# A step of dense matmuls between the copies of a recurrent state and its transpose

## Chip, cores and metric

The kernel runs on one core of a Trainium2 chip. The metric is the device time of one execution in microseconds. Before the change the median of 3 runs is 1598.35 us (1597.43 to 1599.26). The chip's engines are named as in the profile: PE is TensorE (PEld its weight loads), DVE is VectorE, ACT is ScalarE, POOL is GpSimd and SP issues the DMAs.

## The reference

One layer of a hybrid decoder for 1024 tokens of width 1024, in float32: a norm, one input projection, two head groups side by side (retention on 4 heads of 128, RWKV-7 on 8 heads of 64), an output projection, a SwiGLU feed-forward part, a gated embedding and a last norm. What matters here is RWKV-7, whose state of 64 x 64 per head is updated token after token:

```
def step(state, inp):
    r_t, w_t, k_t, v_t, kk_t, b_t = inp
    sa = jnp.einsum('bhvk,bhk->bhv', state, -kk_t)
    state = (state * w_t[:, :, None, :] + sa[..., None] * b_t[:, :, None, :]
             + v_t[..., None] * k_t[:, :, None, :])
    return state, jnp.einsum('bhvk,bhk->bhv', state, r_t)
...
_, y = lax.scan(step, jnp.zeros((B, H, N, N), jnp.float32),
                (tm(r), tm(decay), tm(k), tm(v), tm(kk), tm(kk * a)))
```

The rest is mostly dense products, among them `proj = hn @ w_in`, `mixed @ w_o` and `silu(hf @ w_gate) * (hf @ w_up)`.

## The kernel before

**Dense work.** Each large product of 128 x 512 outputs is a row of matmuls `d` with 512 columns. An operand is split into a high and a low part (`hi`, `lo`, line 250 on ScalarE and line 251 on GpSimd or VectorE), so that every 128 rows of the inner dimension take three matmuls: high x high, high x low, low x high. Such a group of three is called a piece here; `dense` (line 258) is a generator that emits one piece at each call. The tokens are done in two halves of 512.

**The RWKV groups.** `rwkv_group(p, hf)` does two heads (p = 0 to 3) of one half (hf = 0, 1), so there are eight groups in a row. Its 512 tokens are cut into 8 chunks of 64 (`NU`). A group goes through stages: `prep` and `ops` (factors), `A` (products `pb` and the inversion of a triangular matrix by 62 short VectorE instructions in turn, lines 646 and 648), `tok` (products `pk`, transposes `pq`), `mid` (first the products `psm`, whose results ScalarE copies to `hbd` and `Xb`, then `pw` with copies to `Wbd` and `Gbd`, then `pmq` and `pkh`), `chain`, and `fin` (norm of the output, transposes `py` and `pyt`, store of `Y`).

**The chain** (lines 742 to 758) carries the state over the 8 chunks, each step on the one before. A step u writes `pZ` with two products, one from `Vbd` and `KA`, one from the old state `Sn` and `BA`. Then the new state, which stands in two 64 x 64 blocks of `pZ`, is copied to `STb`, one block by ScalarE (line 751) and one by VectorE (line 752). TensorE transposes it (`tr`, line 754, a matmul with the identity, line 196, into `pS`), and ScalarE copies that with a scale into the next `Sn` (line 756). The last chunk of the second half needs no new state, so the transpose runs 8 x 4 + 7 x 4 = 60 times. While a group is in its chain, the next group is in stage `A`: its inversion shares VectorE with the chain's copies.

**The order.** `weave` (line 117) writes the program. A group's generator hands back a stage and a wait, `yield "chain", CHW`; the group's next step is due when the planner's own clock has gone on by the wait times 1.58 in the first half (`WAIT`) and 1.98 in the second (`WAIT1`), and until then `weave` emits dense pieces, or retention tasks that are due. That clock counts a matmul of 512 columns as 512 / 2.4 = 213.3, a piece as 640. Before, the step's products, copies, transpose and copy out are emitted at once, and `CHW = 900` then asks for 1422 (first half) or 1782 (second half), which is three pieces in both. Retention tasks (`rtp`, `rsc`, `rU`, `rY`, `ryt`, lines 793 to 878) are woven in the same way.

What `weave` writes isn't yet the order on the chip: a list scheduler then places each instruction on its engine by priorities and a model of when its inputs are ready. An instruction whose inputs it takes to be late is put behind others that were written after it. Each engine runs its row in that order. SP's row holds all loads and stores, those of weights (`st`) too.

Of the kernel before, what the change touches and what calls it, by code (L numbers as in the profile page):

```python
# [95 lines left out]
MIDW = 9676  # L96
MIDS = 1378
TOKW = 1156
CHW = 900
RLD = 3770  # L100
RROT = 3633
RST = 6253
# [76 lines left out]
def tile_hybrid_layer(ctx: ExitStack, tc: tile.TileContext, I, out):  # L179
# [7 lines left out]
    def mm(ps, lhsT, rhs, start, stop, more=False):  # L187
        n = math.prod(rhs.shape[1:])
        pe[0] += n / 2.4 if rhs.dtype == F32R else 2 * max(107.0, n / 1.2)
        m = nc.tensor.matmul(ps, lhsT, rhs, start=start, stop=stop, skip_group_check=more)  # L190
        tail["mm"] = m.ins
        return m

    def tr(ps, x):
        pe[0] += 109.0
        return nc.tensor.transpose(ps, x, ident)
# [29 lines left out]
    def psa(name):  # L226
        return psr.tile([P, 512], F32, tag="ra", name=name, bufs=2)
# [125 lines left out]
    with ExitStack() as s1:  # L353
# [197 lines left out]
        def flat(t):  # L551
            return t.rearrange("p h t -> p (h t)")
# [3 lines left out]
        def rwkv_group(p, hf):  # L556
# [186 lines left out]
            for u in range(NU):  # L743
                z = pZ[u % 2][:, u // 2]
                first = hf == 0 and u == 0
                mm(flat(z), flat(Vbd[:, u]), flat(KA[:, u]), start=True, stop=first)
                if not first:
                    mm(flat(z), state[p], flat(BA[:, u]), start=False, stop=True)
                if hf == 0 or u < NU - 1:
                    st = STb[:, u % 2]  # L750
                    act(st[0:64, 0, :], z[0:64, 0, :], AF.Copy)
                    V.tensor_copy(st[64:128, 1, :], z[64:128, 0, :])
                    ps = psa("pS")[:, 0:P]
                    tr(ps, flat(st))
                    Sn = sm.tile([P, P], F32, tag=f"S{p}" if u == NU - 1 else "S", name="Sn", bufs=1 if u == NU - 1 else 2)
                    act(Sn, ps, AF.Copy, scale=PC[:, u:u + 1])
                    state[p] = Sn
                yield "chain", CHW

# [537 lines left out]
        for h in range(2):  # L1297
            for k in range(KT):
                tasks[f"mix{h}{k}"] = (mix_load(h, k), 0, ["wo0" if h else "x0free", f"ret{k}{h}" if k < 4 else f"group{k - 4}{h}"])
        weave([(f"group{p}{hf}", rwkv_group(p, hf), need[p]) for hf in range(2) for p in range(4)],  # L1300
              tasks, dg, count, pe, done)

# [242 lines left out]
```

## Time and profile before

| | |
|---|---|
| median of 3 runs | 1598.35 us |
| the profiled execution | 1598.74 us |
| its span, first to last instruction | 1597.0 us |
| TensorE busy | 1497.2 us, 94% |
| VectorE, ScalarE, GpSimd busy | 1203.1, 722.4, 512.7 us |
| mean granted TensorE clock | 0.986 |
| chains of the eight groups | within 186 to 892 us |

The busy time of TensorE is no measure of its speed, since its matmuls overlap and their ends are modelled; what counts is where it stands idle and why. A wait in the profile names the instruction that stood still, and behind the arrow the one that released it.

### The profile page before, as it was taken

What the parts mean: (1) busy time and instruction counts of PE and PEld (TensorE: products, weight loads), DVE (VectorE), ACT (ScalarE), POOL (GpSimd) and SP (SyncE); (2) the same over time, 40 slices, a digit from 0 to 9 for tenths busy, and PEclk for the clock granted to TensorE, in tenths of its full rate; (3) what the DMA queues carried; (4) which work ended last, traced back from release to release, by engine and by line L of the source; (5) the groups of instructions that cost most, each with busy time, mean ns of one, the idle gap of its engine ahead of it and who ended that gap; (6) DMA issues with size and microseconds to landing.
All of it is one profiled execution on the core that took longest, in us unless ns stands there. A gap on an engine that the chain in (4) does not pass through costs nothing.

```text
span 1597.0 us, 21675 instructions
## 1 busy us (share of the span) xinstructions
PE 1497.2 (94%) x7328; PEld 1220.0 (76%) x7328; DVE 1203.1 (75%) x2466; ACT 722.4 (45%) x1442; POOL 512.7 (32%) x389
## 2 busy tenths in 40 slices
PE   6999899998888889989889999999999999999997
PEld 5777768776677767767768877778888888888897
DVE  7668895969889696894875545768888888886675
ACT  6755435353545647445344324543333333334554
POOL 7411111121321122324223340455555555570000
PEclk9999999999999999999999999999999999999998
DMA  6544242242544555335233546332223222331222
GB/s 199 175 154 166 96 129 84 89 152 78 174 133 145 189 165 190 96 105 155 87 127 113 171 119 188 115 121 85 92 90 90 91 93 86 119 93 56 83 91 75
DMA packets 108767, 194.09 MB, mean 122 GB/s; under 512 B 12272, under 2 KB 16496, under 8 KB 108656
## 3 DMA queue, kind: packets, MB, share of 16 engines
q1 hardware_dynamic: 108656, 192.71, 38.0%
q8 instruction: 58, 0.95, 0.2%
q14 instruction: 53, 0.43, 0.1%
HBM read 151.24 MB, written 41.42 MB: 121 GB/s over the span
## 4 chain that ended last, share of the span: by engine, by line
PE 57%; DVE 23%; ACT 7%; DMA 6%; issue 4%; POOL 2%; SPq 0%; ACTq 0%; DVEq 0%; POOLq 0%
PE d L190 31%; PE pd L190 13%; PE pg L190 6%; DVE tmp L646 4%; DVE R L648 3%; DMA st<-in_w_gate_dram 2%; POOL lo L251 2%; DMA st<-in_w_up_dram 1%; DVE lo L251 1%; ACT hi L250 1%; DVE Dm L640 1%; DVE inv L599 1%; PE pkh L190 1%; PE pb L190 1%; ACT BA L685 1%
## 5 line engine op out<-in xcount | busy, mean ns | idle before, releaser
L190 PE MATMUL d<-hT,hi 128*128 128x512 f32 x1408 | 452.0, 401 | 4.1 <-ACT hi L250 4.1
L251 POOL TENSOR_TENSOR lo<-st,hi 128x512 fp32r<-128x512 f32 x173 | 241.8, 1399 | 590.6 <-ACT hi L250 531.3
L190 PE MATMUL d<-x,hi 128*128 128x512 f32 x960 | 319.7, 408 | 8.9 <-ACT x L339 8.0
L190 PEld LDWEIGHTS d<-hT,hi 128*128 128x128 f32 x1408 | 263.5, 192 | 54.9 <-ACT hi L250 5.6
L250 ACT ACTIVATE hi<-st 128x512 fp32r<-128x512 f32 x298 | 187.0, 628 | 258.2 <-PE d L190 96.4
L190 PE MATMUL d<-hT,lo 128*128 128x512 f32 x704 | 279.8, 398 | 5.9 <-DVE lo L251 3.4
L190 PE MATMUL pd<-ring 128*128 128x512 f32 x948 | 260.4, 389 | 0.0
L190 PEld LDWEIGHTS d<-x,hi 128*128 128x128 f32 x960 | 177.1, 192 | 43.3 <-ACT x L339 8.0
L190 PEld LDWEIGHTS pd<-ring 128*128 128x128 f32 x948 | 177.9, 188 | 37.1 <-ACT rm L1145 0.2
L190 PE MATMUL d<-x,lo 128*128 128x512 f32 x480 | 192.9, 402 | 2.8 <-POOL lo L251 2.4
L190 PEld LDWEIGHTS d<-hT,lo 128*128 128x128 f32 x704 | 134.2, 191 | 38.3 <-DVE lo L251 6.3
L251 DVE TENSOR_TENSOR lo<-st,hi 128x512 fp32r<-128x512 f32 x125 | 115.7, 927 | 55.9 <-ACT hi L250 54.9
L1147 DVE TENSOR_TENSOR x<-x,pd 128x512 f32<-128x512 f32 x180 | 118.6, 679 | 26.9 <-PE pd L190 26.9
L251 POOL TENSOR_TENSOR ring<-xr,ring 128x512 fp32r<-128x512 f32 x53 | 73.2, 1386 | 146.5 <-ACT ring L250 67.3
L250 ACT ACTIVATE ring<-rm 128x512 fp32r<-128x512 f32 x87 | 53.8, 629 | 131.3 <-DVE rm L1080 83.8
L190 PEld LDWEIGHTS d<-x,lo 128*128 128x128 f32 x480 | 92.0, 192 | 23.1 <-POOL lo L251 4.7
L646 DVE TENSOR_TENSOR tmp<-Dt,R 128x248 f32<-128x248 f32 (+30 forms) x248 | 89.5, 361 | 3.2
L648 DVE TENSOR_TENSOR R<-R,tmp 128x248 f32<-128x248 f32 (+30 forms) x248 | 83.8, 338 | 3.3
L190 PE MATMUL d<-mix,hi 128*128 128x512 f32 x256 | 82.1, 400 | 0.9 <-ACT hi L250 0.9
L251 DVE TENSOR_TENSOR ring<-rm,ring 128x512 fp32r<-128x512 f32 x65 | 58.4, 902 | 13.0 <-ACT ring L250 12.1
L250 ACT ACTIVATE ring<-xr 128x512 fp32r<-128x512 f32 x57 | 34.9, 625 | 73.8 <-PE pd L190 72.6
L190 PEld LDWEIGHTS d<-mix,hi 128*128 128x128 f32 x256 | 48.1, 192 | 10.8 <-ACT hi L250 1.3
(315 smaller groups left out, 2393.7 us busy)
## 6 DMA issues: line engine op xcount, KB each, us to landing
st<-in_w_gate_dram SPq DMA_DIRECT2D x88, 256.0 KB, 2.9
st<-in_w_up_dram SPq DMA_DIRECT2D x88, 256.0 KB, 2.9
st<-in_w_in_dram SPq DMA_DIRECT2D x86, 256.0 KB, 2.9
xr<-in_w_down_dram SPq DMA_DIRECT2D x44, 256.0 KB, 2.7
retd<-rt SPq DMA_DIRECT2D x32, 256.0 KB, 2.5
rr<-retd SPq DMA_DIRECT2D x32, 256.0 KB, 3.4
st<-in_w_o_dram SPq DMA_DIRECT2D x32, 256.0 KB, 3.0
rkvd<-rkvt SPq DMA_DIRECT2D x24, 256.0 KB, 2.1
```

The costliest lines, as they stand in the source:

```text
L190: m = nc.tensor.matmul(ps, lhsT, rhs, start=start, stop=stop, skip_group_check=more)
L250: act(hi, src, AF.Copy)
L251: return (eng or V).tensor_tensor(out=lo, in0=src, in1=hi.bitcast(F32), op=ALU.subtract)
L599: V.reciprocal(out=inv, in_=inv)
L640: V.tensor_tensor(out=Dm, in0=d0v[:, 0].rearrange("p u t -> p t u").unsqueeze(2).broadcast_to([P, 32, 4, NU]), in1=d0v[:, 1].rearrange("p ...
L646: V.tensor_tensor(out=tmp[:, :, 0:i], in0=Dt[:, i:i + 1, 0:i].broadcast_to([P, 8, i]), in1=R[:, :, i:i + 1].broadcast_to([P, 8, i]), op=AL ...
L648: V.tensor_tensor(out=R[:, :, 0:i], in0=R[:, :, 0:i], in1=tmp[:, :, 0:i], op=ALU.subtract)
L685: act(dst(h)[h * C:(h + 1) * C, j::2, :], pqv[j * C:(j + 1) * C, :, h, :], AF.Copy)
L1147: V.tensor_tensor(out=dst, in0=dst, in1=ps, op=ALU.subtract if name == "P4" else ALU.add)
```

## The change

Behind the two copies the chain's step now ends with a wait of its own, and the wait behind the transpose is shorter. By the planner's clock `CHT = 400` asks for 632 in the first half, one piece, and for 792 in the second, two pieces. `CHW = 500` asks for 790 and 990, two pieces in both. A step so takes three pieces in the first half, as before, and four in the second for three.

```
-CHW = 900
+CHT = 400
+CHW = 500
...
                     st = STb[:, u % 2]
                     act(st[0:64, 0, :], z[0:64, 0, :], AF.Copy)
                     V.tensor_copy(st[64:128, 1, :], z[64:128, 0, :])
+                    yield "chain", CHT
                     ps = psa("pS")[:, 0:P]
                     tr(ps, flat(st))
```

Every engine has the same instructions as before. Their rows are the same up to the first chain and from the last retention transpose on, and differ nearly everywhere between. (The numbers of the lines are one higher from line 100 on, and two higher from line 754 on.)

First place: TensorE in the fourth step of the last group's chain, before and with the change (`pZ<-BA,Sn` is the product with the old state, `pS<-cst,STb` the transpose, `d` dense matmuls, `ryt` a retention transpose).

```order
L190 MATMUL pZ<-KA,Vbd 128x128
L190 MATMUL pZ<-BA,Sn 128x128
L196 MATMUL ryt<-cst,rr 128x128 x4
L190 MATMUL d<-hT_5519,hi 128x512
L196 MATMUL pS<-cst,STb 128x128
L190 MATMUL d<-hT_5519,hi 128x512
L190 MATMUL d<-hT_5519,lo 128x512
L190 MATMUL d<-hT_5519,hi 128x512 x2
L190 MATMUL d<-hT_5519,lo 128x512
```

```order
L191 MATMUL pZ<-KA,Vbd 128x128
L191 MATMUL pZ<-BA,Sn 128x128
L191 MATMUL d<-hT_5511,hi 128x512 x2
L191 MATMUL d<-hT_5511,lo 128x512
L191 MATMUL d<-hT_5511,hi 128x512 x2
L191 MATMUL d<-hT_5511,lo 128x512
L197 MATMUL pS<-cst,STb 128x128
L191 MATMUL d<-hT_5511,hi 128x512 x2
L191 MATMUL d<-hT_5511,lo 128x512
L191 MATMUL d<-hT_5511,hi 128x512 x2
L191 MATMUL d<-hT_5511,lo 128x512
```

Before, one dense matmul and a retention transpose stood ahead of the state's transpose; in the steps around it, three dense matmuls. Now there are six in nearly every step of this group, and six behind it.

Second place: TensorE in stage `mid` of the third group of the second half, before (the next row is the first `pw`) and with the change; then ScalarE's row there with the change, from behind the first two copies to `hbd`.

```order
L190 MATMUL psm<-R,a_180 128x32 x4
L196 MATMUL rtp<-cst,rr 128x128 x3
L190 MATMUL d<-hT_5519,hi 128x512 x2
L196 MATMUL rtp<-cst,rr 128x128
L190 MATMUL psm<-Xd,hbd 128x32 x4
L190 MATMUL d<-hT_5519,lo 128x512
L190 MATMUL d<-hT_5519,hi 128x512 x2
L190 MATMUL d<-hT_5519,lo 128x512
L190 MATMUL d<-hT_5519,hi 128x512 x2
L190 MATMUL d<-hT_5519,lo 128x512
L190 MATMUL d<-hT_5519,hi 128x512 x2
L190 MATMUL d<-hT_5519,lo 128x512
```

```order
L191 MATMUL d<-hT_5511,lo 128x512
L191 MATMUL psm<-R,a_180 128x32 x4
L197 MATMUL rtp<-cst,rr 128x128 x4
L191 MATMUL psm<-Xd,hbd 128x32 x4
L197 MATMUL rtp<-cst,rr 128x128 x4
L191 MATMUL pw<-XR,Xb 128x128 x4
L191 MATMUL rsc<-rr 128x128 x4
L191 MATMUL pw<-XR,Xb 128x128 x4
L191 MATMUL pmq<-BA,Wbd 128x128 x4
L191 MATMUL pkh<-BA,Gbd 128x128 x2
L191 MATMUL rU<-rr 128x128 x3
L191 MATMUL pkh<-BA,Gbd 128x128
```

```order
L251 ACTIVATE mix<-st 128x512
L708 ACTIVATE hbd<-psm 32x4x32 x2
L251 ACTIVATE mix<-st 128x512
L831 ACTIVATE rr<-rtp,cst 128x512
L713 ACTIVATE Xb<-psm 32x4x32 x4
L831 ACTIVATE rr<-rtp 128x512
L724 ACTIVATE Wbd<-pw 64x4x64 x2
L724 ACTIVATE Gbd<-pw 64x4x64 x2
L724 ACTIVATE Wbd<-pw 64x4x64 x2
L724 ACTIVATE Gbd<-pw 64x4x64 x2
L611 ACTIVATE ta<-ta,par 128x512
L251 ACTIVATE hi<-st 128x512 x2
```

Before, dense matmuls `d` stand between the products of the stage. Now the whole stage, with tasks of a retention head (`rtp`, `rsc`, `rU`), stands in one row, and the dense product goes on behind it. The high part of its next weights (`hi<-st`) stands on ScalarE behind all copies of the stage, and the first copies of `psm` stand around two splits of `mix`, whose data is the output of earlier groups, read back from memory. Between `pyt` of the group before and this `psm` there were 36 dense matmuls, and now there are 23.

Third place: TensorE at the two transposes `rtp` of the third retention head of the second half, before and with the change; both transposes write the same PSUM bank, which ScalarE copies out between them (line 829).

```order
L190 MATMUL d<-hT_5519,hi 128x512 x2
L190 MATMUL d<-hT_5519,lo 128x512
L196 MATMUL rtp<-cst,rr 128x128 x8
L196 MATMUL pyt<-cst,yn 128x128
L190 MATMUL d<-hT_5519,hi 128x512 x2
```

```order
L197 MATMUL pq<-cst,AR 128x128 x4
L197 MATMUL rtp<-cst,rr 128x128 x3
L191 MATMUL d<-hT_5511,hi 128x512 x2
L191 MATMUL d<-hT_5511,lo 128x512
L191 MATMUL d<-hT_5511,hi 128x512 x2
L191 MATMUL d<-hT_5511,lo 128x512
L191 MATMUL d<-hT_5511,hi 128x512 x2
L191 MATMUL d<-hT_5511,lo 128x512
L191 MATMUL d<-hT_5511,hi 128x512 x2
L191 MATMUL d<-hT_5511,lo 128x512
L197 MATMUL rtp<-cst,rr 128x128 x4
L191 MATMUL psm<-R,a_180 128x32 x4
```

Before, the second four stood right behind the first four; now 12 dense matmuls are between.

## Rows read from the trace of the kernel before

**Rows 1.** The page's busy times by engine: us (share of the span) and instructions.
```profile
PE 1497.2 (94%) x7328; PEld 1220.0 (76%) x7328; DVE 1203.1 (75%) x2466; ACT 722.4 (45%) x1442; POOL 512.7 (32%) x389
```

**Rows 2.** TensorE's waits, 180 to 960 us: instruction <- releaser: us, times, longest.
```profile
PE pS L196 <- DVE STb L752: 18.2, 22, 1.7
...
PE ryt L196 <- ACT rr L871: 4.8, 2, 3.3
PE rtp L196 <- ACT rr L829: 4.2, 1, 4.2
```

**Rows 3.** Windows, fourth and eighth chain: length, each engine's busy us, clock, DMA.
```profile
451.00:482.00 31.00, 25.59 (x148) 19.36 (x146) 30.00 (x81) 12.63 (x35) 9.71 (x6) 1.00 0.34 109
...
868.00:892.00 24.00, 23.32 (x122) 18.43 (x121) 10.31 (x19) 9.11 (x23) 7.46 (x6) 1.00 0.38 119
```

**Rows 4.** Timeline, last group's fifth step: start, us, engine, line, operation [idle <- releaser].
```profile
881.63 0.39 PE L190 MATMUL pZ<-BA,Sn 128*128 128x128 f32 x2
...
881.77 0.70 PE L190 MATMUL d<-hT,hi 128*128 128x512 f32 x2
...
882.30 0.23 DVE L752 COPY STb<-pZ 64x64 f32<-64x64 f32 x1 [2.18 <-ACT STb L751]
882.31 0.40 PE L190 MATMUL d<-hT,lo 128*128 128x512 f32 x1
...
882.58 0.33 PE L196 MATMUL pS<-cst,STb 128*128 128x128 f32 x1
```

**Rows 5.** Timeline, a step of the first group at 207 us.
```profile
207.38 0.34 DVE L646 TENSOR_TENSOR tmp<-Dt,R 128x176 f32<-128x176 f32 x1
...
207.50 1.35 POOL L251 TENSOR_TENSOR lo<-st,hi 128x512 fp32r<-128x512 f32 x1 [10.21 <-ACT hi L250]
...
207.75 1.30 DVE L648 TENSOR_TENSOR R<-R,tmp 128x176 f32<-128x176 f32 x1
...
209.08 0.23 DVE L752 COPY STb<-pZ 64x64 f32<-64x64 f32 x1
...
209.37 0.33 PE L196 MATMUL pS<-cst,STb 128*128 128x128 f32 x1 [1.06 <-DVE STb L752]
```

**Rows 6.** TensorE's waits as in rows 2, 186 to 482 us, then 538 to 892.
```profile
PE pS L196 <- DVE STb L752: 12.0, 12, 1.7
...
PE pS L196 <- DVE STb L752: 6.2, 10, 1.2
```

**Rows 7.** Timeline, TensorE at the third middle stage of the second half.
```profile
702.87 0.60 PE L196 MATMUL pyt<-cst,yn 128*128 128x128 f32 x4
...
718.82 0.97 PE L190 MATMUL psm<-R,a 128*128 128x32 f32 x8
...
721.51 0.73 PE L190 MATMUL d<-hT,hi 128*128 128x512 f32 x2 [1.36 <-ACT hi L250]
...
722.64 1.08 PE L190 MATMUL psm<-Xd,hbd 128*128 128x32 f32 x8 [0.29 <-ACT hbd L707]
...
724.07 1.05 PE L190 MATMUL d<-hT,hi 128*128 128x512 f32 x2
...
725.35 1.05 PE L190 MATMUL d<-hT,hi 128*128 128x512 f32 x2
...
731.43 0.62 PE L190 MATMUL d<-hT,hi 128*128 128x512 f32 x2
...
732.11 0.62 PE L190 MATMUL d<-hT,hi 128*128 128x512 f32 x2
```

**Rows 8.** Timeline, ScalarE at the same place.
```profile
720.04 0.63 ACT L250 ACTIVATE mix<-st 128x512 fp32r<-128x512 f32 x1 [0.79 <-DMA st<-mixd]
...
721.49 1.11 ACT L707 ACTIVATE hbd<-psm 32x128 f32<-32x128 f32 x4
723.76 1.12 ACT L712 ACTIVATE Xb<-psm 32x128 f32<-32x128 f32 x4 [1.17 <-PE psm L190]
...
728.63 0.38 ACT L723 ACTIVATE Wbd<-pw 64x256 f32<-64x256 f32 x1 [1.62 <-PE pw L190]
```

More of the change, by code (lines that the diff above doesn't have):

```diff
@@ L98 @@
 TOKW = 1156
-CHW = 900
+CHT = 400
+CHW = 500
 RLD = 3770
@@ L752, in rwkv_group @@
                     V.tensor_copy(st[64:128, 1, :], z[64:128, 0, :])
+                    yield "chain", CHT
                     ps = psa("pS")[:, 0:P]
```

## Prediction

> **What bounds the kernel now.** I read the page's busy times first, then TensorE's waits, then the stretches in which the state's chain runs, and last the timeline of single steps. TensorE is busy for 1497.2 of the span's 1597.0 us [rows 1]. The change adds and drops no instruction on any engine; it only moves them, from the first product of the first chain to the last retention transposes, all of it between 180 and 960 us. So the time can change only by what TensorE stands idle, or runs at a lower clock, in that stretch. Its longest wait there is that of the state's transpose, which stands for VectorE's half of the copy, 18.2 us in 22 waits [rows 2]. The chain's stretches show the same: in the fourth group of the first half TensorE is busy for 25.59 of 31 us while VectorE is busy for 30, and in the last group of the second half for 23.32 of 24 us with VectorE at 10.31 [rows 3]. The chain hurts where VectorE is full.
>
> How one step runs. In the last group the product with the state starts at 881.63, the copies end at 882.53 and the transpose starts at 882.58; with three dense matmuls between there is nothing to wait for [rows 4]. At 207 us the same step, with four dense matmuls between in the order, still waits 1.06 us: the VectorE instruction ahead of the copy, a subtraction of the inversion (L648), takes 1.30 us where its neighbour takes 0.34, beside a GpSimd instruction of 1.35 us, and the copy begins at 209.08 [rows 5]. So the latency of an unhindered step is already covered by the one piece that the scheduler puts there by itself. What is left to gain is in copies that are late in VectorE's queue.
>
> What the idle times mean. A dense matmul is shown 0.40 us long, but three start in 0.68 us (731.43 to 732.11), one each 0.23 us [rows 7]. A wait is counted from the shown end, so a true delay is 0.17 us longer than its row. First half: 12.0 us in 12 waits [rows 6], with 12 x 0.17 that is 14.0. Second half: 6.2 in 10, so 7.9. The other 38 of the 60 transposes can hide up to 0.17 us each, 6.5 at most; I take 3.
>
> **The sum, part by part.**
>
> 1. Second half of the tokens. The planner needs two pieces for the new wait and two for the old one there (the section on the change), four a step for three. In the order of instructions, the dense matmuls between the product with the state and the transpose are, over the 28 steps after each group's first, 125 before and 170 now: 1.6 more a step, 0.37 us. The ten waits are 0.79 us each on average. With 0.37 us more cover they lose 3.7 us; with the three more (0.69 us) that most steps get, 6.9. I take 6, since the added three are the rule in the order and the mean comes from a few steps that get none, and 1 of the hidden delays: **-7** (ends -3 and -9). The pieces themselves cost nothing, as the dense work is the same in total; they are taken from the stretches between the chains. The chains end later, the last one by 54 dense matmuls (12 us), but the last retention transpose still comes at the same place in the dense work, and the output projection behind it too.
>
> The row on the late copy bears on a rule. The Trainium skill, page "SBUF — State Buffer", section "SBUF: two separate sides", says that VectorE and GpSimd share a pair of ports as an exclusive lock: a VectorE instruction with two SBUF inputs waits for a whole GpSimd instruction. The trace agrees with 1.30 us for 0.34 [rows 5]. By that rule a piece of 0.69 us covers about half of such a block, and the ten waits would give back no more than the 6.9 above.
>
> 2. First half. One piece for the new wait, two for the old one: three as before, and the scheduler had dense work in front of the transpose already. The counts fall, from 162 to 140 over 28 steps; without the outliers of 17 and 12, and of 8 and 5 in the same places, 133 and 127. That takes 0.05 to 0.18 us of cover from each step, so 12 waits grow by 0.6 to 2.2: **+1**. Ends: all waits go, because the copies fall elsewhere (-14), or all 28 steps pay 0.18 (+5).
>
> 3. The middle stage of the third group of the second half. Before, 12 dense matmuls stand between its first product (psm) and its first pw; now there is none from psm to the last pkh, and the next weights' high part stands on ScalarE behind all of the stage's copies (second place in the section on the change). Its cost: ScalarE's work up to there is four hbd (1.11), four Xb (1.12), eight Wbd and Gbd (3.04) and five copies of 128x512 (mix, mix, two retention copies, ta; 0.63 each, 3.15), 8.4 us [rows 8]. The mix copy between the hbd copies waits for a load; before it began 17.2 us after pyt (702.87 to 720.04) [rows 7, 8], and now psm comes some 3.0 us earlier after pyt, with 23 dense matmuls between for 36. TensorE's own products there are about 60 starts of 0.1 us (psm: eight in 0.97), 6.0 us. Idle: 8.4 + 3.0 - 6.0 = 5.4. After the gaps of 1.36 and 0.29 us the matmuls run at half pace there, three in 1.28 us (724.07 to 725.35) for 0.68, for two such pieces: the clock at 1.2 for 2.4 GHz, 1.2 us. That comes again, so 6.6, less what the place loses already (1.36 + 0.29 + 2 x 0.17 + 1.2 = 3.2): **+3.4**. Ends: 0, if the load is in time and copies overlap more; +10.6, if nothing overlaps and the clock falls twice (8.4 + 3.0 + 2 x 1.2 - 3.2).
>
> On the clock the rule and this row weigh the same way, but it is the reason why this stall is dear: the Trainium skill, page "TensorE: Matmul & The Clock Gate", section "What's actually happening", says that the throttled clock is the default and activity releases it.
>
> 4. The first group of the second half has the same in small: the last psm is now followed at once by eight pw where 10 dense matmuls stood. The Xb copies (1.12) are open: **+1** (0 to +2.7, with four Wbd and Gbd copies of 0.38).
>
> 5. Two retention transposes in one PSUM bank stood back to back and waited 4.2 us for the copy out [rows 2]. Now 12 dense matmuls (2.8 us) stand between: **-3** (0 to -4.4).
>
> 6. The other waits between 180 and 960 us fall anew, since the rows of each engine stand differently; single lines of them are about 5 us [rows 2]. Zero, with 5 us to either side.
>
> Sum: -7 + 1 + 3.4 + 1 - 3 = **-4.6 us**. The profiled execution took 1598.74 us (its span and 1.7 us around it), 0.4 above the median of the runs shown, 1598.35; against the median that gives 1593.8. A measurement of this kernel can tell about 0.2%, 3.2 us, from no change.
>
> **Rivals.**
>
> A. The wait moves along. The copy stands in VectorE's queue by the same scheduler that places the transpose, and where the transpose comes later, so may the copy. For it: the step at 207 us has one matmul more of cover than the one at 881 us, and waits all the same [rows 4, 5]; the block by GpSimd is longer than a piece. Against it: in the last group, with VectorE half idle, nothing moves the copy. Then term 1 is -2, the sum +0.4, the time 1598.8.
>
> B. The uncovered middle stages eat the gain. Place: terms 3 and 4. Without them the sum is -9. With both at their high ends (10.6 + 2.7) it is +4.3: 1602.7, slower. It decides from a net price of 9 us on for no gain, of 12.2 for slower by 0.2%. For it: in the order there is no other work for TensorE. Against it: ScalarE and TensorE do overlap in the same stage today, with 0.29 us left open before the second psm [rows 7].
>
> C. The first half gains too: the transpose has its own step now, and if half of its 14.0 us go, term 2 is -7 and the time 1585.8.
>
> **Chances and range.** Forecast 0.55 (its own range 1588 to 1599: the ends of terms 1, 3 and 5, hardly all on one side), A 0.20, B 0.15, C 0.10. Faster by over 0.2% means below 1595.2, which lies above the forecast's middle: 0.39 of the forecast's 0.55, C's 0.10 and 0.03 of A, 0.52. Within 0.2%: 0.14 of the forecast, 0.14 of A, 0.02 of B, 0.30. Slower: 0.02 of the forecast, 0.03 of A, 0.13 of B, 0.18. The range reaches from C to B: 1585 to 1603.
>
> **What would show it.** Right: the wait of the transpose for the copy falls from 6.2 to under 3 us in the second half and stays near 12 in the first; a TensorE gap of several us in the third group's middle stage, with a granted clock below 1 there; the wait of the retention transpose gone. Wrong: the second half still waits 5 us or more (A), first-half waits under 7 us (C), or gaps of over 9 us in the two middle stages (B).

## The result, and the profile after

The change made the kernel slower: 1613.33 us (median of 4 runs, 1612.57 to 1613.73) against 1598.8 us (4 runs, 1597.43 to 1604.58) beside it; the ratio is 1.0077, 95% interval 1.0051 to 1.0103. The prediction was 1593.8 us with a range to 1603. The profiled execution took 1612.57 us, its span is 1610.8 us, 13.8 more than in the profile before.

The busy line of the page after, to set against [rows 1], shows where it is not: TensorE's busy time grew by 3.3 us only.

```profile
PE 1500.5 (93%) x7328; PEld 1231.0 (76%) x7328; DVE 1213.6 (75%) x2466; ACT 722.3 (45%) x1442; POOL 509.2 (32%) x389
```

TensorE's waits after, first from 180 to 960 us (against [rows 2]), then from 180 to 540 and from 540 to 985 (against [rows 6]); us in total, times, longest:

```profile
PE pS L197 <- DVE STb L753: 20.4, 21, 2.2
PE pyt L197 <- DVE yn L781: 18.6, 5, 7.0
...
PE pS L197 <- DVE STb L753: 9.5, 10, 2.0
...
PE pyt L197 <- DVE yn L781: 16.4, 3, 7.0
PE pS L197 <- DVE STb L753: 10.9, 11, 2.2
```

The state's transpose waits as long as before, 20.4 for 18.2 us. In the second half, where I expected under 3 us, it is 10.9 for 6.2. And a wait is in the list that was not worth a line before: pyt, the transposes behind the output norm, stand 16.4 us for VectorE's yn in the second half (1.0 us before). The retention transpose's 4.2 us [rows 2] are gone, and so is ryt's line.

**Why the transpose still waits.** A step of the sixth group's chain after, on TensorE, VectorE and GpSimd:

```profile
684.87 1.33 POOL L1009 TENSOR_TENSOR g<-g,R 128x512 f32<-128x512 f32 x1 [1.57 <-DVE g L1008]
685.10 1.31 DVE L647 TENSOR_TENSOR tmp<-Dt,R 128x192 f32<-128x192 f32 x1
...
685.60 0.39 PE L191 MATMUL pZ<-BA,Sn 128*128 128x128 f32 x2
...
687.20 1.38 POOL L252 TENSOR_TENSOR lo<-st,hi 128x512 fp32r<-128x512 f32 x1 [1.00 <-ACT hi L251]
...
687.62 1.16 DVE L649 TENSOR_TENSOR R<-R,tmp 128x184 f32<-128x184 f32 x1
...
689.33 0.23 DVE L753 COPY STb<-pZ 64x64 f32<-64x64 f32 x1
...
689.61 0.33 PE L197 MATMUL pS<-cst,STb 128*128 128x128 f32 x1 [1.77 <-DVE STb L753]
```

Eight dense matmuls start between the product (685.60) and the transpose and are done 2.2 us behind it. The copy, though, starts 3.73 us behind it. VectorE isn't idle: it works through the next group's inversion (L647, L649), two of whose instructions take 1.31 and 1.16 us beside GpSimd's of 1.33 and 1.38, and through retention's states. The mean over the 28 steps of the second half shows it plainly. Between the product with the old state and the transpose stand 4.46 dense matmuls before and 6.07 after, 0.37 us more at 0.2275 us each (three start in 0.68 us [rows 7]); the copy starts 1.51 us behind that product before and 1.88 after, 0.37 us more too. In the first half, over the 28 steps that have an old state, both fall: 5.79 to 5.00 matmuls (0.18 us), and 2.03 to 1.83 us (0.20). On average the copy moved along with its transpose, both ways.

Moving along would cost nothing if all steps were alike. But a step whose copy is later than its cover stands still, and a step with more cover than it needs gives nothing back. Behind each group's first transpose there are 24 stretches from product to transpose in the second half. With TensorE's own work taken off they lose 10.2 us before and 15.3 after, and the growth is in the late steps: four stretches of over 1 us make 4.8 us before, six make 10.3 after. The step above is one of the six.

**Why pyt waits.** TensorE at the sixth group's output after, then VectorE's row of the norm behind py there, from the start of the square root to yn:

```profile
698.93 0.60 PE L197 MATMUL py<-cst,Y 128*128 128x128 f32 x4
...
717.07 0.39 PE L191 MATMUL d<-hT,hi 128*128 128x512 f32 x1
724.49 1.09 PE L197 MATMUL pyt<-cst,yn 128*128 128x128 f32 x4 [7.03 <-DVE yn L781]
...
726.23 1.05 PE L191 MATMUL d<-hT,hi 128*128 128x512 f32 x2
```

```profile
710.57 0.15 DVE L305 TENSOR_SCALAR fs<-fs 128x8 int32<-128x8 int32 x1
...
714.57 0.69 DVE L1016 SCALAR_TENSOR_TENSOR g<-g,d 128x512 f32<-128x512 f32 x1
...
715.25 1.22 DVE L689 TENSOR_TENSOR Xb<-Xd,cst 128x1024 f32<-128x1024 f32 x1
...
717.18 1.24 DVE L693 COPY R<-R 32x128 f32<-32x128 f32 x1
...
719.10 1.23 DVE L693 COPY R<-R 32x128 f32<-32x128 f32 x1
...
721.50 0.16 DVE L311 SCALAR_TENSOR_TENSOR fs<-fs 128x8 f32<-128x8 f32 x1
722.24 2.10 DVE L781 TENSOR_SCALAR yn<-py,fs 128x64 f32<-128x64 f32 x8
```

The same row in the kernel before (each line number one lower in the square root, two at yn):

```profile
691.27 0.16 DVE L304 TENSOR_SCALAR fs<-fs 128x8 int32<-128x8 int32 x1
...
695.87 0.34 DVE L779 TENSOR_SCALAR yn<-py,fs 128x64 f32<-128x64 f32 x1
```

The norm is a string of tiny dependent instructions, and whatever stands between two of them delays all. Before, the square root took from 691.27 to yn's start at 695.87, 4.6 us, with short ends of the next group's inversion in between. After, it took 11.7 us (710.57 to 722.24): the chain is longer now, py comes later against the next group's inversion, and the square root falls where the inversion has ended and the long instructions behind it (Xb, the copies of L693, dense epilogues) fill its gaps. The two copies of L693 are long because of GpSimd: beside its instructions of 1.27 and 1.26 us they take 1.24 and 1.23, where the copies of L694, of the same size, take 0.21. TensorE's row has 73 dense matmuls between py and pyt there (54 before), runs out of them at 717.46 and stands for 7.03 us. The next matmuls then run at half pace, two of them 1.05 us long for 0.62 at the full clock [rows 7]: the granted clock is 1.00 from 715 to 720 us and 0.50, the lower of its two levels, from 720.2 to 730.2. So the stall costs more than its row. By the Trainium skill, page "TensorE: Matmul & The Clock Gate", section "What's actually happening", an idle array falls back to the lower clock. The trace agrees here: the fall to 0.50 lies inside the stall.

### The profile page after: what moved, and what is told of

Same layout as the page of the kernel before. It is cut to its first block, busy times and chain, and to the rows that moved or that the text cites. A ratio compares the mean times of both kernels' runs of the same rounds, so it can differ in the third digit from the quotient of the medians.

```text
span 1610.8 us, 21661 instructions
## 1 busy us (share of the span) xinstructions
PE 1500.5 (93%) x7328; PEld 1231.0 (76%) x7328; DVE 1213.6 (75%) x2466; ACT 722.3 (45%) x1442; POOL 509.2 (32%) x389
## 4 chain that ended last, share of the span: by engine, by line
PE 56%; DVE 20%; ACT 5%; DMA 3%; issue 3%; POOL 1%; SPq 0%; DVEq 0%; ACTq 0%; POOLq 0%
PE d L191 30%; PE pd L191 13%; PE pg L191 6%; DVE R L649 4%; DVE tmp L647 4%; POOL lo L252 1%; DVE lo L252 1%; DMA st<-mixd 1%; DVE Dm L641 1%; ACT XR L686 1%; DMA st<-in_w_up_dram 1%; PE pw L191 1%; DVE yn L781 1%; PE pb L191 1%; ACT Vbd L686 1%
## 5 line engine op out<-in xcount | busy, mean ns | idle before, releaser
L252 POOL TENSOR_TENSOR lo<-st,hi 128x512 fp32r<-128x512 f32 x173 | 236.0, 1367 | 622.8 <-ACT hi L251 491.3
L647 DVE TENSOR_TENSOR tmp<-Dt,R 128x248 f32<-128x248 f32 (+30 forms) x248 | 90.0, 363 | 3.8
L649 DVE TENSOR_TENSOR R<-R,tmp 128x248 f32<-128x248 f32 (+30 forms) x248 | 88.8, 358 | 3.8
L252 DVE TENSOR_TENSOR ring<-rm,ring 128x512 fp32r<-128x512 f32 x65 | 60.7, 937 | 12.5 <-ACT ring L251 11.6
```

The lines of the kernel that those rows point to most:

```text
L252: return (eng or V).tensor_tensor(out=lo, in0=src, in1=hi.bitcast(F32), op=ALU.subtract)
L647: V.tensor_tensor(out=tmp[:, :, 0:i], in0=Dt[:, i:i + 1, 0:i].broadcast_to([P, 8, i]), in1=R[:, :, i:i + 1].broadcast_to([P, 8, i]), op=AL ...
L649: V.tensor_tensor(out=R[:, :, 0:i], in0=R[:, :, 0:i], in1=tmp[:, :, 0:i], op=ALU.subtract)
```

## The experiments

All have the kernel before run beside them on the same chip, and the ratios are against it. Beside the waits I read each trace by TensorE's marks, the instructions that every version has: the first and the last state transpose of a group, py and pyt. From a mark's start I take off TensorE's own work that stands ahead of it in the order (0.2275 us a dense matmul, about 0.22 a product, 0.09 a transpose); what is left is idle time and lost clock. For the sixth group's chain, say, the first and last transposes are 20.98 us apart before (656.84 to 677.82) with 48 dense matmuls between, and 24.43 us after (668.10 to 692.53) with 57: 24.43 - 20.98 - 9 x 0.2275 = +1.4. The table gives such growths against the kernel before, in us: up to the end of the first half's last group; the four chains of the second half; from a chain's end to its pyt (the norm), four times; and from a pyt to the next chain (the middle stages), four times. The last columns are the median time of each version and the ratio. f3 left no trace to compare and is not in the table.

Two cautions. The growths are of one profiled execution each, and executions of one kernel lie up to 15 us apart (the kernel before beside h1, sixteen from 1592.3 to 1607.1), so a single growth of 1 to 3 us says little. And a ratio is known to some 0.002 or 0.003 either way, so the difference of two ratios to some 0.003 or 0.004; where ± stands below, it is worked out from the two intervals.

| version | first half | chains | norm | middle | us | ratio [95%] |
|---|---|---|---|---|---|---|
| the change | -2.1 | +5.8 | +6.5 | +6.8 | 1613.3 | 1.0077 [1.0051, 1.0103] |
| e1 three pieces, split | -1.0 | -1.6 | +1.1 | +13.7 | 1605.1 | 1.0063 [1.0040, 1.0086] |
| e2 four pieces, no split | +3.4 | +11.2 | -0.6 | +4.2 | 1614.1 | 1.0104 [1.0067, 1.0141] |
| e3 split in first half only | -1.4 | -0.3 | -0.3 | -0.6 | 1596.9 | 1.0005 [0.9990, 1.0020] |
| e4 split in second half only | -1.2 | +5.9 | +5.7 | +1.4 | 1608.9 | 1.0081 [1.0055, 1.0107] |
| e5 change, norm raised | -2.5 | +5.1 | -10.0 | +4.3 | 1597.2 | 1.0012 [0.9993, 1.0031] |
| e9 change, pyt later | -2.6 | +4.9 | -2.2 | +11.8 | 1611.2 | 1.0094 [1.0067, 1.0120] |
| e7 change, copy raised | +0.1 | +5.5 | +6.0 | +3.2 | 1613.6 | 1.0097 [1.0065, 1.0129] |
| e8 change, both raised | +5.3 | +7.4 | -8.2 | +11.6 | 1610.3 | 1.0074 [1.0053, 1.0096] |
| f0 before, norm raised | -0.2 | -1.1 | -9.2 | +5.3 | 1592.2 | 0.9976 [0.9957, 0.9995] |
| f1 e1, norm raised | +1.2 | -0.9 | -5.9 | +12.1 | 1599.2 | 1.0017 [1.0002, 1.0031] |
| f2 e2, norm raised | -1.3 | +7.7 | -8.1 | +10.3 | 1608.8 | 1.0080 [1.0051, 1.0109] |
| g1 f0, bonus raised | +1.4 | -1.2 | -9.2 | +7.2 | 1596.4 | 0.9997 [0.9983, 1.0011] |
| g2 e5, bonus raised | -2.9 | +5.5 | -9.9 | +8.6 | 1598.9 | 1.0012 [0.9999, 1.0024] |
| g3 f0, two pieces | -0.9 | 0.0 | -6.3 | +10.5 | 1602.5 | 1.0035 [1.0012, 1.0058] |
| h1 change, copy on ScalarE | -5.5 | +0.8 | +9.9 | +3.0 | 1607.8 | 1.0063 [1.0043, 1.0084] |
| h2 f0, copy on ScalarE | -6.1 | -3.3 | -9.4 | +9.7 | 1588.9 | 0.9952 [0.9930, 0.9975] |
| h3 e5, copy on ScalarE | -5.1 | +1.6 | +0.7 | +4.2 | 1597.2 | 0.9999 [0.9976, 1.0022] |

### Which half, and split or length

The change does two things at once: a piece now stands ahead of the transpose, and in the second half a step has four pieces for three. The first four kernels take these apart.

```diff
@@ e1, in the change
-CHT = 400
+CHT = 320
@@ e2, in the kernel before
-CHW = 900
+CHW = 1000
@@ e3, in the change (e4: hf == 1 in both places)
-                    yield "chain", CHT
+                    if hf == 0:
+                        yield "chain", CHT
...
-                yield "chain", CHW
+                yield "chain", CHW if hf == 0 else 900
```

> CHT = 320 for 400: the split stays, but a step takes 1 + 2 pieces in both halves, three as before the change. Theory 1 (the fourth piece of the second half moves the chains' ends behind the next group's inversion, and the output norm's transposes pyt then wait for VectorE): the waits of pyt in the second half fall from 16.4 us (4.25 + 7.03 + 5.08) to under 4, the time to 1596 to 1604. Theory 2 (the split itself does it, by what the scheduler makes of a transpose that is due later): pyt still waits over 10 us, time 1610 to 1615.

> The kernel before with CHW = 1000 for 900: no split, three pieces a step in the first half and four in the second. Theory 1: the pyt waits of the second half come to 10 us or more, time 1604 to 1612. Theory 2: pyt waits as before, about 1 us in the second half, time 1596 to 1601.

> The change in the first half alone; the second half has one wait of 900 as before. Theory 1: what the change lost in time up to the first chain of the second half (4.7 us ahead at the end of the fourth chain, 2.4 behind at the start of the fifth) stays, the pyt waits of the second half are under 4 us: time 1598 to 1603. Theory 2: the first half bears a share of the loss by its number of steps, 32 of 60: 1605 to 1608, with pyt waits in the first half too.

> The change in the second half alone (four pieces a step there, with the split). Theory 1: no difference until the fifth chain, then pyt waits of 10 us or more in the second half, time 1605 to 1612. Theory 2: a share of 28 of 60 steps, 1604 to 1607, and no group of waits that stands out.

e3 is no different from the kernel before, e4 is as slow as the change: the loss is made in the second half. e2, four pieces without the split, is at least as slow, and slower than either theory had it. Its waits in the second half:

```profile
PE pS L196 <- DVE STb L752: 14.0, 9, 3.2
PE pyt L196 <- DVE yn L779: 7.7, 2, 5.0
```

So the fourth piece is enough to lose, in the chain above all (+11.2). e1 has the split with three pieces and loses nothing in its chains (-1.6), yet stands at 1.0063: its 13.7 us are in the middle stages, spread over several waits. Neither theory fits it, with 1605 us and 7.2 us of pyt waits (1.8 for yn, 5.4 for an instruction of the inversion). That loss was not followed further. So the split alone is enough to lose as well, and the two losses don't add up, since the change has both and stands at 1.0077.

### The norm raised, the norm later, the copy raised

```diff
@@ e5, in the change: from here to yn, all of it indented
+            with tc.high_priority(3000 if hf else 0):
                 for i in range(8):
                     V.bn_stats(out=bst[:, i, :], in_=py[:, i * C:(i + 1) * C])
...
@@ e9, in the change
-            yield "fin", FINW
+            yield "fin", FINW + (2400 if hf else 0)
@@ e7, in the change (e8: e5 and e7 together)
+                    with tc.high_priority(3000):
                         V.tensor_copy(st[64:128, 1, :], z[64:128, 0, :])
```

> The change, with the output norm's VectorE instructions (bn_stats to yn, ahead of the pyt transposes) raised above everything else in the order, in the second half only. The chain's four pieces and TensorE's order in the second half stay nearly as in the change (63, 60, 63, 66 dense matmuls between py and pyt against 63, 73, 63, 66). Theory W (the loss is pyt waiting for a norm that stands in VectorE's row among the next group's long instructions): pyt's waits in the second half fall from 16.4 us to under 3, and the time falls by 10 to 16 us, to 1598 to 1603. Theory P (the loss is the longer chain itself, its pS and pZ waits, or work pushed to the end): pyt's waits fall or not, the time stays at 1609 to 1615, because what VectorE does first for the norm it does later for the next group's inversion, and pq, pS or pmq wait instead.

> The change, with the pyt transposes set 2400 units (12 dense matmuls by the planner's own price) later behind py in the second half: 81, 81, 81 and 78 dense matmuls between them against 63, 73, 63 and 66. VectorE's instructions are not raised. Theory W: the added cover, 18, 8, 18 and 12 matmuls of 0.2275 us, is 4.1, 1.8, 4.1 and 2.7 us, so the waits of 4.25, 7.03 and 5.08 us fall to about 0.2, 5.2 and 1.0, that is from 16.4 to about 6.4 us, and the time by about 10 us to 1601 to 1606. Theory P: the time stays at 1609 to 1615.

> The change, with VectorE's half of the state copy raised above everything else in the order, so that it no longer stands behind the next group's inversion; nothing is raised in the norm. Theory A (pS still waits in the change because the copy stands as late in VectorE's row as its transpose in TensorE's): pS's waits fall from 20.4 us in the two halves to under 8, and TensorE's order shows 9 to 12 dense matmuls in nearly each step. Theory W says that this leaves most of pyt's 16.4 us in the second half, so the time falls by 6 to 12 us only, to 1601 to 1607. Theory P (the chain's waits are the whole loss) says 1596 to 1600. If the copy waits for TensorE's pZ and not for its place in the row, the pS waits stay at 18 us or more and the time at 1611 to 1615.

> The change with both: the state copy raised in both halves, the output norm in the second half. If W and A are both right their gains add: pyt's waits in the second half under 3 us, pS's under 8 in all, and a time of 1588 to 1596, at or below the kernel before. If the two only shift VectorE's delay to the inversion and what stands behind it, other waits (pq, pb, psm, rY, bo) take at least half of it and the time is 1600 to 1610.

e5 takes the ratio from 1.0077 to 1.0012. Its TensorE waits in the second half, then VectorE and TensorE at the sixth group's norm:

```profile
PE pS L197 <- DVE STb L753: 11.4, 12, 2.1
PE bo L191 <- DVE hs L252: 6.2, 2, 3.2
PE bo L191 <- ACT hs L251: 4.5, 3, 3.1
```

```profile
700.09 2.09 DVE L782 TENSOR_SCALAR yn<-py,fs 128x64 f32<-128x64 f32 x8
...
706.09 0.60 PE L197 MATMUL pyt<-cst,yn 128*128 128x128 f32 x4
```

yn begins 9.4 us behind py (690.66) for 23.3 in the change and 13.1 before, pyt waits for nothing there, and TensorE's order in the second half is almost the change's. pS's waits are what they were. So the norm's place in VectorE's row looks like most of the loss; the controls below take back a part of that.

e9 misses its expectation. pyt's waits fall from 16.4 to 4.9 us as worked out, but the time does not follow: the middle stages lose 11.8 us (for 6.8), with bo and psm in the list now.

```profile
PE bo L191 <- ACT hs L251: 6.0, 2, 3.1
PE pyt L197 <- DVE yn L781: 4.9, 1, 4.9
PE psm L191 <- ACT hbd L708: 3.5, 2, 3.0
```

Setting TensorE's instruction later only moves the place where it stands: VectorE's row is as late as before. e7 misses the other way. The copy was raised above everything, and TensorE's order got 9 to 12 dense matmuls in nearly each step, but pS's waits stay (12.2 us in the second half). The copy starts 1.74 us behind the product on average for 1.88, with 5.25 dense matmuls for 6.07 between, so it gained no more than its cover lost. The time is that of the expectation's last case, but the copy does not wait for pZ: in 23 of the 28 steps VectorE goes to it straight from another instruction. A step of e7:

```profile
804.83 1.38 POOL L1010 TENSOR_TENSOR g<-g,R 128x512 f32<-128x512 f32 x1 [2.69 <-DVE g L1009]
...
804.97 0.39 PE L191 MATMUL pZ<-BA,Sn 128*128 128x128 f32 x2
...
805.09 1.36 DVE L647 TENSOR_TENSOR tmp<-Dt,R 128x216 f32<-128x216 f32 x1
...
806.16 1.41 POOL L252 TENSOR_TENSOR lo<-st,hi 128x512 fp32r<-128x512 f32 x1
...
806.48 1.33 DVE L649 TENSOR_TENSOR R<-R,tmp 128x216 f32<-128x216 f32 x1
...
808.67 0.23 DVE L754 COPY STb<-pZ 64x64 f32<-64x64 f32 x1
...
808.95 0.33 PE L197 MATMUL pS<-cst,STb 128*128 128x128 f32 x1 [2.20 <-DVE STb L754]
```

Instructions of the inversion stand in front of the copy all the same, and two of them take 1.36 and 1.33 us for some 0.38 each, beside GpSimd's of 1.38 and 1.41. A raise sets the order of the row; that the scheduler's model still put the inversion first, and VectorE then ran later than the model, is my reading, which no run tests. The Trainium skill, page "SBUF — State Buffer", section "SBUF: two separate sides", says that VectorE and GpSimd share one pair of ports as an exclusive lock. That fits the pairs of rows shown here.

e8, both raises, has no pyt waits left and is slow again (1.0074): it loses in the first half and in the middle stages what e5 does not. I can't say why these two differ so much; it was not followed.

### Controls for the raise

```diff
@@ f0: the kernel before; f1: e1; f2: e2; f3: e3; each with e5's edit
+            with tc.high_priority(3000 if hf else 0):
                 for i in range(8):
...
```

> The kernel before with the output norm's VectorE instructions raised in the second half, as in e5, and nothing of the change. It is the control for e5. Theory W (the change's loss is the norm that comes late in VectorE's row, and the kernel before has hardly any of it: 1.0 us of pyt waits in its second half): the raise has nothing to win here, 1593 to 1600 us. Rival G (the raise is worth 12 to 16 us in any version, so that e5 says nothing about the change): 1581 to 1588.

> e1 (the copies, one piece, the transpose, two pieces) with the norm raised in the second half. e1 had 7.2 us of pyt waits there and stood at 1605. Theory W: these go, 1595 to 1600. Rival D (the split itself costs in the second half, beside the norm): 1602 to 1607.

> e2 (four pieces behind the transpose in the second half, no split) with the norm raised there. e2 had 7.7 us of pyt waits and 14.0 us of pS waits in the second half and stood at 1614. Theory W: pyt's waits go and the time falls by 8 to 14 us to 1600 to 1606, more than the pyt waits alone since other waits followed from them. Rival D2 (four pieces cost in another way, through the stretch where the pieces run out): 1609 to 1615.

> e3 (the split in the first half alone, at 1597 us) with the norm raised in the second half. Theory W: 1592 to 1599, no different from e3, with 1.1 us of pyt waits to win. If the raise is worth more by itself (rival G): 1581 to 1588, and this would be a version faster than both kernels.

The raise is worth something in any version: f0 is faster than the kernel before (0.9976), f3 as well (1594.19 us, 0.9979 [0.9962, 0.9996]). So e5 shows less than it seemed to. In the change the raise is worth 0.0065, in the kernel before 0.0024; the difference, 0.0041 (±0.0037) or 6.6 us, is what the change had made the norm late, and TensorE's marks say 6.5. e5 against f0 leaves 0.0036 (±0.0027), 5.8 us, and the marks of the chains differ by 6.2 (+5.1, -1.1). Each pair agrees better than its interval would promise. f2 stays at 1.0080: four pieces without the split lose 7.7 us in their chains however early the norm is, so theory W falls there. f1 takes the time that theory W gave it, but stands 0.0041 (±0.0024) above f0, so rival D is not refuted: the split with three pieces costs in the second half beside the norm too. Set side by side, the ratios of the versions with three and with four pieces a step in the second half:

| second half | three pieces | four pieces |
|---|---|---|
| no split | 1 (before) | 1.0104 (e2) |
| split | 1.0063 (e1) | 1.0077 (the change) |
| no split, norm raised | 0.9976 (f0) | 1.0080 (f2) |
| split, norm raised | 1.0017 (f1) | 1.0012 (e5) |

Without the split the fourth piece costs 0.0104 in both pairs. With the split it costs nothing that can be told from noise, and with the norm raised the split takes back 0.0068 (±0.0035) of what the fourth piece costs. Why the two don't add up is not shown. f0's waits show what comes next:

```profile
PE bo L190 <- DVE hs L251: 7.9, 3, 3.9
PE pS L196 <- DVE STb L752: 6.0, 9, 1.2
```

### What is left: the bonus, the pieces, the copy

```diff
@@ g1, in f0, and g2, in e5: raised is 3000 for headsum(bo, kp) in the second half, else 0
-                split(t, hi, lo)
+                with tc.high_priority(raised):
+                    split(t, hi, lo)
@@ g3, in f0
-                yield "chain", CHW
+                yield "chain", 600 if hf else CHW
@@ h1, in the change, h2, in f0, and h3, in e5
-                    V.tensor_copy(st[64:128, 1, :], z[64:128, 0, :])
+                    act(st[64:128, 1, :], z[64:128, 0, :], AF.Copy)
```

> f0 (the kernel before, norm raised in the second half) with the two instructions that split the bonus's product (hi on ScalarE, lo on VectorE, ahead of the two bo matmuls) raised there as well. f0 has 7.9 us of bo waits in 3 in its second half. If the bonus is what the raised norm pushes back: bo's waits fall to under 3 us and the time by 3 to 6 us to 1586 to 1590. If VectorE is simply behind there and the wait moves to the next instruction that TensorE needs (pq, ss, psm): no change, 1590 to 1595.

> e5 (the change, norm raised) with the bonus's split raised in the second half. e5 has 10.7 us of bo waits there. Theory K (what is left of the change's loss is its chain, 5 us of pS waits more than in the kernel before): it gains as much as g1 over f0 and stays 3 to 7 us above g1, 1590 to 1597. Theory L (what is left is the bonus): it comes within 2 us of g1.

> f0 with a chain step of two pieces of dense matmuls in the second half in place of three. If more pieces a step make the loss (a longer chain, the dense epilogues in front of the copy), fewer should win or at least not lose on that account: pS's waits per step stay at 0.2 to 0.4 us, py comes 5 to 8 us earlier, and the time is 1588 to 1594. If cover is what counts, the transpose has about one matmul less before it, pS's waits rise from 6.0 to 9 us or more, and dense work that is left over moves behind the groups: 1593 to 1600.

> The change with VectorE's half of the state copy on ScalarE too, behind the other half, so that the transpose waits for nothing on VectorE. Theory A (the transpose waits because its copy moves along in VectorE's row): pS's waits fall from 20.4 us to under 5, the chains win 5 us or more in the second half and about 8 in the first, and with pyt's waits left the time falls to 1599 to 1605. If ScalarE's row is as late (its 128x512 copies take 0.63 us), pS waits for ScalarE in place of VectorE, 10 us or more, and the time stays at 1608 to 1614.

> f0 (the kernel before with the norm raised in the second half, 1592) with both halves of the state copy on ScalarE. Theory A: the kernel before has 18.2 us of pS waits; under 5 are left, and 6 to 12 us of the time go, the rest falling back on the inversion and the norm that TensorE waits for next: 1580 to 1586, faster than both kernels. If the waits move to ScalarE: 1590 to 1596.

> e5 (the change with the norm raised, 1597) with both halves of the copy on ScalarE. Theory A: what the split and the fourth piece cost in the chain was the copy, so this comes within 3 us of h2, 1580 to 1588. If the fourth piece costs by its length alone, it stays 4 to 7 us above h2.

The bonus is not it: g1 and g2 win nothing, bo waits as before (7.8 and 10.7 us). The chains still differ by 6.7 us (+5.5, -1.2), though the times do by 2.5 us only. Fewer pieces don't win either: g3's chains stand at 0.0 for f0's -1.1, and the time is worse. Without the split three are enough, four lose in the chains, two lose elsewhere.

The copy on ScalarE is the direct test of the late copy. In h1 the chains of the second half come to +0.8 for the change's +5.8 (and the first half's four chains alone to -12.6 for -0.9), so by the marks the chain's loss was the copy in VectorE's row. pyt stays, as it must; and pS now waits for ScalarE, in a few steps:

```profile
PE pyt L197 <- DVE yn L781: 14.7, 3, 7.2
PE pS L197 <- ACT STb L753: 6.9, 3, 3.4
```

The time, 1607.8 us, lies 3 us above what I expected of it; part of the gain is lost again outside the chains. h2 is the fastest version of the study, 1588.9 us, 0.9952 of the kernel before: three pieces, no split, the norm raised in the second half, the copy on ScalarE. Against f0 it is faster by 3.2 us, where I expected 6 to 12, and the two intervals overlap; its waits in the second half have moved to the dense weights' high part and the bonus:

```profile
PE d L190 <- ACT hi L250: 8.4, 4, 4.0
PE bo L190 <- DVE hs L251: 6.6, 2, 4.3
...
PE pS L196 <- ACT STb L752: 0.8, 4, 0.3
```

h3, the change with both, was to come within 3 us of h2, or 4 to 7 above it if length alone costs, and stays 8.3 above it (5 us apart in the chains, 10 in the norm's stretch). It is no faster than e5. Here ScalarE is the late row: pZ waits for the state's copy out of PSUM.

```profile
PE pZ L191 <- ACT Sn L758: 5.2, 5, 2.8
PE pS L197 <- ACT STb L753: 4.6, 3, 3.5
```

So the split and the fourth piece together lose in each pair that was run (the change against before, e5 against f0, g2 against g1, h3 against h2), by 2.5 to 14.5 us, and not always in the same place; g2 against g1 is within the noise. With the norm raised and the copy moved in both kernels 0.0047 (±0.0032) of the change's 0.0077 is left. The late copy and the late norm are where TensorE stands in the change. They are not the whole of its time: when they are put right, other rows are late.

## Why the prediction was wrong

**Term 1, -7 us, failed, and with the sign.** It read the transposes' new places from the order (1.6 matmuls more cover a step, and the trace shows the same) and credited that cover in full to copies that it left where they were. The copies moved by 0.37 us for 0.37 us of cover; the chains lost 5.8 us where they were to win 7, and the transposes waited 10.9 us where under 3 was the sign of being right. The check was to hand: in the same order the copy's place in VectorE's row could be read beside the transpose's. Rival A named the mechanism and had it right, but still gave the term a gain of 2 us. What it gave as the reason against (in the last group, with VectorE half idle, nothing moves the copy) is right for that group and holds for it alone: there the transposes lose 0.9 us as before, and the 1.3 us that the chain lost are one product's wait for ScalarE's Sn.

**Term 6, zero, failed: the pyt wait, +6.5 us.** It stood at "the other waits fall anew". The text itself said that the chains end later, and let only TensorE's row follow from that. VectorE's row behind py, the norm among the next group's inversion, was never looked at, since pyt waited 1 us before.

**Term 2, +1.** The first half lost 2.1 us less up to its last pyt, its pS waits went from 12.0 to 9.5. The cover fell as counted; the copies fell with it. Within its ends.

**Term 3, +3.4.** After, the third group's middle stage waits in two places, with the order as foreseen:

```profile
740.57 1.91 PE L191 MATMUL psm<-Xd,hbd 128*128 128x32 f32 x8 [1.26 <-ACT hbd L708]
...
749.86 0.71 PE L191 MATMUL pkh<-BA,Gbd 128*128 128x128 f32 x4 [0.74 <-ACT Gbd L724]
```

The marks give +2.0 for that stretch: right in kind and dear by 1.4 us. Rival B's gaps of over 9 us are not there. The load that was to hold up the mix copy was in time.

**Term 4, +1, was too small: the first group's middle stage lost 4.6 us, beyond the term's end of 2.7.** The pw behind the last psm do wait for the Xb copies, as foreseen, but for 3.07 us. ScalarE, then TensorE:

```profile
523.95 0.63 ACT L251 ACTIVATE hi<-st 128x512 fp32r<-128x512 f32 x1 [1.10 <-DMA st<-in_w_ple_up_dram]
524.61 1.12 ACT L713 ACTIVATE Xb<-psm 32x128 f32<-32x128 f32 x4
```

```profile
525.49 3.68 PE L191 MATMUL pw<-XR,Xb 128*128 128x128 f32 x16 [3.07 <-ACT Xb L713]
```

The term priced the copies alone (1.12). In ScalarE's new row they stand behind a split of dense weights that waits 1.10 us for its load. Before, they ran from 517.20 to 518.85, ahead of that split, and the pw waited for nothing. It is the kind of wait that term 3 feared of the mix copy, in another place.

**Term 5, -3.** The retention transpose no longer waits; right.

What is left of the sum: the middle stages of the second and the last group changed by +0.3 and -0.1 us, and behind the last pyt 3.2 came back. With 6.8 for all four middle stages, -2.1 + 5.8 + 6.5 + 6.8 - 3.2 = 13.8, the difference of the spans.

The range ended at 1603 because each rival was the forecast's own account with one term changed. None let a stage that did not wait before begin to wait.

## What to carry to other kernels

Cover that a change puts in front of a waiting instruction is worth something only if the instruction it waits for stays where it is, so read both rows of the new order before a gain is counted. Where a chain is made longer, look at the strings of short dependent instructions on VectorE that follow it, and at what the order now sets between them; raising such a string was worth 0.24% even in the kernel that did not show it as a wait. Where an awaited copy stands in a full row, an engine with room can take it: that and the raise made the fastest version here, while in the change the same move made ScalarE the late row. And where a change does two things, run each alone: here each of them lost by itself.

## What the runs showed of the hardware

In the rows here, what a VectorE instruction takes beside GpSimd's hangs on GpSimd's instruction and hardly on its own size. The inversion's, on 192 elements a partition, took 1.31 us (685.10). In the change at 704 us, GpSimd's split and an instruction of the square root on four elements a partition, which takes 0.15 us alone (705.87):

```profile
703.75 1.38 POOL L252 TENSOR_TENSOR lo<-st,hi 128x512 fp32r<-128x512 f32 x1 [0.20 <-ACT hi L251]
...
703.90 1.25 DVE L309 TENSOR_TENSOR rmisc<-rmisc 128x4 f32<-128x4 f32 x1
```

I had reckoned with such blocks for the inversion's instructions of 0.34 us; for a norm of some thirty tiny ones each block lasts as long as eight of them.
